# V stored from full transposes, even chunks first, and LayerNorms 2 and 3 with statistics of transposed blocks, in a hybrid encoder layer

## The chip, the core and the metric

The kernel runs on one core of one Trainium2 chip. The metric is the device time of one execution in microseconds (us). The core has a matrix engine (TensorE, PE in the rows), a vector engine (DVE), a scalar engine (ACT), GpSimd (POOL), and a sync engine (SP), from which nearly all transfers of this kernel are issued. Each engine works through its own instructions in order and waits for the others at semaphores.

## The reference

One encoder layer is applied to two groups of requests, each a sequence of 512 tokens with 1024 features, with shared weights, in float32.

```
x = LN(alpha*x + 0.5*SwiGLU_1(x))
h = x @ W_in                       # columns of MLA, of RWKV-7 and of two gates
A = MLA(h_q, h_kv) @ P_mla ; B = RWKV7_bidir(h_rwkv) @ P_rwkv
x = LN(alpha*x + (sig(g_A)*A + sig(g_B)*B) @ W_o)      # LayerNorm 2
x = LN(alpha*x + CrossAttn(x, LN(mem)))                # LayerNorm 3
x = LN(alpha*x + 0.5*SwiGLU_2(x))

# RWKV-7, forward and backward in time, a state S of 64x64 in each of 8 heads
Sa = S @ a_t
S  = S * w_t + outer(Sa, b_t) + outer(v_t, k_t)
y_t = S @ r_t
```

The LayerNorm takes mean and variance of each token over its 1024 features.

## The kernel before

Activations lie transposed: features on the 128 partitions, the 512 tokens of a group along the free axis, so that 1024 features are eight tiles ("rows") of 128x512 per group. A product in nearly full precision is three matmuls of rounded operands: each operand is split into a high and a low part (`xh`, `xl` for activations, `whl` for both parts of a weight), and `Bank.prod` issues high*high, high*low and low*high into one PSUM bank. `Bank.mm` is L215 of the profile, `Bank.tr`, a transpose on PE against the identity `cc`, is L220. The eight PSUM banks go round under three tags, four under "a", two each under "b" and "c". `split` makes the two parts, by a cast on ACT and a subtraction on DVE or GpSimd; `whl` rows are those of weights.

The stages follow each other: SwiGLU 1 (0 to about 700 us, with LayerNorm 1), the projections and MLA (to about 1212), the recurrence (to about 1765), the gated mix (to 1800), W_o with LayerNorm 2 (to 1925), cross attention with LayerNorm 3 (to about 2069), SwiGLU 2 and LayerNorm 4.

The stage before the recurrence runs over four pairs of heads `h` (64 features of each of two heads fill the 128 partitions; a pair is called a head below, as its code counts them so). For each it projects k, r and v for both groups, and between the projections `attend` runs the softmax attention of MLA, whose tiles are `sm_p` and `pt`. The tile of v (`t`, in the rows `sh`, the shifted projection) and its copy with time reversed (`tr`, in the rows `sq`) are turned by `crossed` (L249): the two 64-row halves `e` of the tile are handled apart, chunk by chunk of 64 tokens, the lower half by a matmul with the identity and the upper half by a transpose, so that the halves change places. A copy on DVE or ACT takes the bank to `st`, which is stored to `d_v`.

The recurrence works on eight chunks of 64 tokens. For each head, `front` (L1612) loads v into `uv` (zero in the halves that a block structure leaves out), and r, k, the decays and so on into three `ld` tiles for each group; ACT takes exponentials of the decays (`pp`, `ip`), DVE multiplies them in (`ar`, `bk`), and PE forms `phi`. Then a triangular inverse is built by DVE (`dw`, `tm`, `lw`), turned (`xt`, `ct`) and finished on PE and ACT (`qt`). `chunks` (L1751) runs the eight chunks in turn, each with a state `gs` and `sn`. `sums_in` (L1837) loads v once more (`vt`) and the gate (`gt`), and `sums` applies the head's normalization and gate. Between all these steps `fill` takes pieces of other work, `beside`: projections for the branch gates with their weights `wraw`, whose results `t` are stored to `d_gate`, the memory's projections, and MLA's output.

LayerNorms 2 and 3 are objects of `RowNorm` (L366): each finished row is squared on ACT and added to two running sums, the plain one on GpSimd for group 0 and on DVE for group 1, the squares on DVE (`ln_s`). `stats` multiplies both sums by a column of 1/1024 on PE. LayerNorms 1 and 4 use `BlockNorm` (L394), whose loop is

```
for j in range(4):
    b = Bank(k, self.tags[0])
    for i in range(4):
        b.tr(b.t[:, i * P : i * P + P], self.y(4 * half + i)[:, j * P : j * P + P], k.ident)
    nc.vector.bn_stats(out=self.bn[:, j, half], in_=b.t)
```

so half of a token's features (four rows) is turned into one bank for each block of 128 tokens, and DVE takes its statistics. `Norm.spread` turns mean and rstd back into rows.

`FfnWeights` loads and splits the weights of a SwiGLU, with sums of them for a fast matrix product; `ahead(n)` makes the next n of them early.

The order of instructions on each engine isn't the program's. A scheduler lays the instructions out by simulated times, buffers and priorities, and a change in one place can move others nearby. Waits are on the data and on buffers becoming free; SP's transfers are issued one after the other in its order.

## Time and profile before

| what | value |
|---|---|
| median of 3 runs | 2743.46 us (2743.14 to 2744.37) |
| profiled execution | 2749.23 us, span 2747.4 us |
| granted clock of PE over the span | 0.971 |
| instructions | 41481 |
| PE busy | 2597.5 us, 95% |
| DVE busy | 2118.7 us, 77% |
| ACT busy | 1090.2 us, 40% |
| chain that ended last | PE 54%, DVE 11%, ACT 3%, DMA 2% of the span |

A row of a timeline gives the start from the span's beginning, the duration, the engine, the line of the program, the operation, the tile written and the tiles read, shapes, a count of like instructions, and in square brackets the idle time in front with what ended it. PE's instructions are pipelined, so durations of neighbours overlap; the distance from one start to the next is what a piece takes. SPq rows are the issue of transfers on SP's queue. The row of a group has the count, the sum of the busy time and the mean in ns, then the idle time in front. A window's row has its start and end, its length, the busy time of PE, of its weight loads, DVE, ACT and POOL (with counts), the granted clock, the share of the transfer engines and GB/s.

### The profile page before, as it was taken

The numbers are of one execution on the slowest core, as the hardware profiler recorded it, in microseconds if no ns is written. First come the engines' busy times: TensorE is split into PE (matmuls) and PEld (weight loads), VectorE is DVE, ScalarE is ACT, GpSimd is POOL, SyncE is SP. The second block draws the span as 40 slices with busy tenths as digits, with TensorE's granted clock in tenths as the row PEclk, the third lists the DMA queues.
The fourth block names the chain that finished last, engine by engine and source line by source line (L and its number), as shares of the span: only waits on it lengthen the run. The fifth ranks groups of instructions, "written<-read, shape, count | busy, mean of one in ns | idle before, by whom it ended". The sixth has DMA issues, their size and how long they took to land.

```text
span 2747.4 us, 41481 instructions
## 1 busy us (share of the span) xinstructions
PE 2597.5 (95%) x15600; PEld 2074.1 (75%) x15600; DVE 2118.7 (77%) x3745; ACT 1090.2 (40%) x2004; POOL 699.2 (25%) x479
## 2 busy tenths in 40 slices
PE   8999999999999999997989888999999999999996
PEld 7888887787767777776677676777777888887784
DVE  7888887999466777758475768657788888887988
ACT  5344332222453555444443433224554433342222
POOL 0233332443200001133123331103031323232443
PEclk9999999999999999998999898999999999999998
DMA  4344337671244333343434353541102433347751
GB/s 173 123 154 161 146 135 297 237 264 64 92 171 157 114 97 112 115 139 136 132 110 128 119 179 116 166 157 46 47 31 81 165 143 139 141 173 266 275 200 65
DMA packets 164200, 396.08 MB, mean 144 GB/s; under 512 B 41056, under 2 KB 47456, under 8 KB 164000
## 3 DMA queue, kind: packets, MB, share of 16 engines
q1 hardware_dynamic: 164000, 393.43, 40.9%
q8 instruction: 124, 2.03, 0.3%
q14 instruction: 76, 0.62, 0.1%
HBM read 259.41 MB, written 133.96 MB: 143 GB/s over the span
## 4 chain that ended last, share of the span: by engine, by line
PE 54%; DVE 11%; issue 3%; ACT 3%; DMA 2%; POOL 1%; SPq 0%; POOLq 0%; ACTq 0%; DVEq 0%
PE ps L215 51%; PE ps L220 3%; DVE whl L179 1%; DVE dw L179 1%; DVE x L179 1%; DVE z L179 1%; DVE rs L179 1%; DVE phi L179 1%; DVE tm L179 1%; DVE ln_s L179 1%; DMA ld<-d_rw 1%; DVE wt L179 0%; ACT whl L245 0%; DMA d_q<-st 0%; POOL ln_z L357 0%
## 5 line engine op out<-in xcount | busy, mean ns | idle before, releaser
L215 PE MATMUL ps<-xo,whl 128*128 128x512 f32 x3792 | 899.3, 396 | 14.1 <-DVE z L179 8.5
L215 PE MATMUL ps<-xh,whl 128*128 128x512 f32 x2688 | 889.3, 402 | 15.7 <-ACT xh L245 11.4
L215 PEld LDWEIGHTS ps<-xo,whl 128*128 128x128 f32 x3792 | 712.9, 189 | 185.7 <-DVE z L179 6.7
L215 PEld LDWEIGHTS ps<-xh,whl 128*128 128x128 f32 x2688 | 508.1, 190 | 132.0 <-ACT xh L245 13.0
L215 PE MATMUL ps<-xl,whl 128*128 128x512 f32 x1344 | 536.5, 399 | 1.4 <-POOL xl L246 1.4
L179 DVE TENSOR_TENSOR whl<-wraw,whl 128x512 fp32r<-128x512 f32 (+4 forms) x269 | 280.4, 1052 | 53.2 <-ACT whl L245 52.7
L245 ACT CAST whl<-wraw 128x512 fp32r<-128x512 f32 (+4 forms) x314 | 219.7, 711 | 247.2 <-PE ps L215 226.4
L215 PEld LDWEIGHTS ps<-xl,whl 128*128 128x128 f32 x1344 | 255.9, 190 | 56.4 <-POOL xl L246 2.7
L712 POOL TENSOR_TENSOR s<-s,up 128x512 f32<-128x512 f32 x80 | 116.4, 1455 | 624.0 <-DVE up L179 399.7
L245 ACT CAST whl<-wt 128x512 fp32r<-128x512 f32 (+3 forms) x280 | 148.5, 555 | 272.5 <-PE ps L215 160.7
L179 DVE TENSOR_TENSOR whl<-wt,whl 128x512 fp32r<-128x512 f32 (+3 forms) x280 | 215.5, 791 | 11.5 <-ACT whl L245 11.4
L246 POOL TENSOR_TENSOR whl<-wraw,whl 128x1024 fp32r<-128x1024 f32 x45 | 109.4, 2433 | 385.8 <-ACT whl L245 353.3
L245 ACT CAST hop<-s 128x512 fp32r<-128x512 f32 x128 | 79.5, 621 | 246.1 <-POOL s L712 180.3
L179 DVE TENSOR_TENSOR hop<-s,hop 128x512 fp32r<-128x512 f32 x128 | 121.4, 949 | 58.3 <-ACT hop L245 50.7
L179 DVE SCALAR_TENSOR_TENSOR x<-ps,x 128x512 f32<-128x512 f32 x184 | 124.5, 683 | 53.6 <-PE ps L215 53.0
L179 DVE TENSOR_TENSOR wt<-wraw 128x512 f32<-128x512 f32 (+3 forms) x140 | 109.9, 785 | 1.0
L179 DVE TENSOR_TENSOR wt<-wraw,wt 128x512 f32<-128x512 f32 (+3 forms) x140 | 102.8, 734 | 4.6 <-DMA wraw<-in_wf_dram 2.6
L610 POOL TENSOR_TENSOR x<-x,s 128x512 f32<-128x512 f32 x48 | 70.6, 1476 | 129.4 <-DVE x L179 129.4
L246 POOL TENSOR_TENSOR xl<-x,xh 128x512 fp32r<-128x512 f32 x48 | 66.8, 1420 | 98.2 <-ACT xh L245 97.9
L179 DVE TENSOR_TENSOR p<-ps,p 128x512 f32<-128x512 f32 x120 | 82.2, 685 | 7.2 <-PE ps L215 4.0
L610 POOL TENSOR_TENSOR x<-x,z 128x512 f32<-128x512 f32 x48 | 71.2, 1485 | 52.8 <-DVE x L179 49.2
L215 PE MATMUL ps<-mh,whl 128*128 128x512 f32 x256 | 81.1, 397 | 1.3 <-ACT whl L245 1.3
(328 smaller groups left out, 3715.9 us busy)
## 6 DMA issues: line engine op xcount, KB each, us to landing
d_h<-hop SPq DMA_DIRECT2D x140, 512.0 KB, 2.6
xo<-d_h SPq DMA_DIRECT2D x140, 512.0 KB, 7.2
wraw<-in_wf_dram SPq DMA_DIRECT2D x95, 512.0 KB, 3.4
wraw<-in_wa_dram SPq DMA_DIRECT2D x57, 512.0 KB, 3.5
wraw<-in_wb_dram SPq DMA_DIRECT2D x32, 512.0 KB, 3.4
wraw<-in_wf_dram SPq DMA_DIRECT2D x36, 384.0 KB, 3.7
ld<-d_rw SPq DMA_DIRECT2D x24, 512.0 KB, 4.8
d_gate<-t SPq DMA_DIRECT2D x32, 256.0 KB, 2.3
```

Of the source, the lines that this page charges most:

```text
L179: inst = f(*args, **kw)
L215: self.last = order(k.tc, k.nc.tensor.matmul(out, a, b, start=start, stop=stop), self.last)
L220: self.last = order(self.k.tc, self.k.nc.tensor.transpose(out, a, ident), self.last)
L245: nc.scalar.copy(hi, src)
L246: (low or nc.vector).tensor_tensor(out=lo, in0=src, in1=hi.bitcast(F32), op=ALU.subtract)
L610: eng.tensor_tensor(out=y[r, c], in0=y[r, c], in1=u, op=ALU.add)
L712: nc.gpsimd.tensor_tensor(out=s[:, i], in0=s[:, i], in1=up[:, i], op=ALU.mult)
```

## The change

The turned v is made by four full 128x128 transposes in place of `crossed`. A block of 128 tokens holds two chunks, an even one on the lower partitions and an odd one on the upper. The copy to `st` reorders the free axis so that the two halves `e` of the features come apart, each with its four blocks. As the halves of one chunk's pair no longer lie on opposite partitions, the loads of `uv` and `vt` go by the parity `r` of the chunk: 16 loads of 64x256 in place of 8 of 64x512 for `uv`, and 8 of 64x4x64 in place of 2 of 128x8x64 for `vt`. In `uv` the even chunks come first; `AT` says where a chunk stands, and `chunks` reads `uv[..., AT[i]]` for `uv[..., i]`.

LayerNorms 2 and 3 become `BlockNorm`s, with the tags "c" for the turned blocks and "b" or "c" for the spread rows in LayerNorm 2, and "a" or "c" and "b" or "c" in LayerNorm 3. A half is added when its fourth row is done. The pool of SwiGLU 2's weight sums is opened earlier, and three of its weights are asked for within the second group's rows of cross attention.

```diff
-class RowNorm(Norm):
-    def add(self, n):
-        nc, y = self.k.nc, self.y(n)
-        if n == 0:
-            self.s1, self.s2 = self.tile("ln_s1", 2), self.tile("ln_s2", 2)
-        sq = self.tile("sq", 4) if n else self.s2
-        nc.scalar.activation(out=sq, in_=y, func=AF.Square)
-        if n:
-            eng = nc.gpsimd if self.tags[0] == "c" else nc.vector
-            eng.tensor_tensor(out=self.s1, in0=self.s1 if n > 1 else self.y(0), in1=y, op=ALU.add)
-            nc.vector.tensor_tensor(out=self.s2, in0=self.s2, in1=sq, op=ALU.add)
-    def stats(self):
-        k, nc, sb = self.k, self.k.nc, self.sb
-        st = Bank(k, self.tags[0])
-        for o, t in enumerate((self.s1, self.s2)):
-            for b in range(4):
-                st.mm(st.t[:, 4 * o + b : 4 * o + b + 1], t[:, b * P : b * P + P], k.mean)
-        m = sb.tile([P, 3, 4], F32, name="ln_m", tag="ln_m", bufs=2)
-        mean, var, sq = m[:, 0], m[:, 1], m[:, 2]
-        nc.vector.tensor_copy(m[:, 0:2], st.t[:, 0:8].rearrange("p (a b) -> p a b", b=4))
-        nc.vector.scalar_tensor_tensor(out=sq, in0=mean, scalar=-1.0, in1=mean, op0=ALU.mult, op1=ALU.mult)
-        nc.vector.scalar_tensor_tensor(out=var, in0=sq, scalar=LN_EPS / ALPHA**2, in1=var, op0=ALU.add, op1=ALU.add)
-        Norm.spread([self], mean, var)
@@ -1186,11 +1156,14 @@
                     t = shifted(proj(w, g), 5 + 3 * h)
                     tr = tmp("sq", 2)
                     nc.scalar.copy(tr, t[:, ::-1])
+
                     for d, src in ((0, t), (1, tr)):
                         b = aux()
-                        crossed(b, k, lambda e, c: src[64 * e : 64 * e + 64, c * C : c * C + C])
+                        for i in range(4):
+                            b.tr(b.t[:, i * P : i * P + P], src[:, i * P : i * P + P], k.ident)
                         vt = tmp("st", 2)
-                        (nc.scalar.copy if d else nc.vector.tensor_copy)(vt, b.t)
+                        (nc.scalar.copy if d else nc.vector.tensor_copy)(
+                            vt.rearrange("p (e b v) -> p e b v", e=2, v=C), b.t.rearrange("p (b e v) -> p e b v", e=2, v=C))
                         nc.sync.dma_start(out=d_v[h][g][:, d], in_=vt)
                     attend(3)
@@ -1309,21 +1282,23 @@
     y32 = keep.tile([P, G, KT, T], F32, name="x32")
     x32 = [y32[:, g] for g in range(G)]
-    def norms_of(i):
-        return [RowNorm(k, sb, lambda n, g=g: x32[g][:, n], f"ln{i}_g", f"ln{i}_b", "cb"[g] * 2) for g in range(G)]
+    def norms_of(i, *tags):
+        return [BlockNorm(k, sb, lambda n, g=g: x32[g][:, n], f"ln{i}_g", f"ln{i}_b", tags[g]) for g in range(G)]
     for q in range(4):
         for g in range(G):
             nc.sync.dma_start(out=x32[g][:, 2 * q : 2 * q + 2], in_=d_x1[g][:, 2 * q : 2 * q + 2])
+    ow = ctx.enter_context(pool("ow", "right"))
     wb_pool = cross.enter_context(pool("wb", "right"))
     st.use((wp, 3, 2), (wb_pool, 2, 0), (wp, 3, 2), (wb_pool, 2, 0), (wp, 3, 2))
     def sum_row(norm, g, n, b, f):
         y = x32[g][:, n]
         nc.vector.scalar_tensor_tensor(out=y, in0=b.t, scalar=f, in1=y, op0=ALU.mult, op1=ALU.add)
-        norm.add(n)
-
-    norms = norms_of(2)
+        if n % 4 == 3:
+            norm.add(n // 4)
+
+    norms = norms_of(2, ("c", "b"), ("c", "c"))
     w = []
     def mix_rows(g, ns):
@@ -1340,11 +1315,11 @@
         for g in range(G):
             mix_rows(g, range(n0, n0 + 4))
             if (n0, g) == (4, 0):
-                norms[0].stats()
+                BlockNorm.stats(norms[:1], False)
     x2 = [None, None]
     for g in range(G):
         if g:
-            norms[g].stats()
+            BlockNorm.stats(norms[1:], False)
         x2[g] = (acts if g else others)(KT, "x")
         norms[g].apply(x2[g])
@@ -1430,22 +1405,23 @@
     kvs[1] = memory_of(1)
     xo[1] = acts(4, "co")
     w = [st.blocks(4) for _ in range(KT)]
-    norms = norms_of(3)
+    norms = norms_of(3, ("a", "b"), ("c", "c"))
     both(attend(1), out_rows(0))
-    norms[0].stats()
-    for _ in out_rows(1):
-        pass
+    BlockNorm.stats(norms[:1], False)
+    fw = FfnWeights(k, wf2, [(wp, 3)] * 3 + [(ow, 1)], [(wp, 2)] * 2 + [(ow, 1)], ow)
+    for i, _ in enumerate(out_rows(1)):
+        if i % 4 == 3 and i > 4:
+            fw.ahead(1)
     x3 = [None, None]
     for g in range(G):
         if g:
-            norms[g].stats()
+            BlockNorm.stats(norms[1:], False)
         x3[g] = acts(KT, "x")
         norms[g].apply(x3[g])
     cross.close()
-    ow, of = ctx.enter_context(pool("ow", "right")), ctx.enter_context(pool("of"))
-    fw = FfnWeights(k, wf2, [(wp, 3)] * 3 + [(ow, 1)], [(wp, 2)] * 2 + [(ow, 1)], ow)
+    of = ctx.enter_context(pool("of"))
     ln = []
     def sums2():
 ...
+    AT = (0, 4, 1, 5, 2, 6, 3, 7)
@@ -1619,9 +1597,10 @@
         self.ar = []
         for g in range(G):
             for d in range(2):
-                src = self.d_v[h][g][:, d].rearrange("p (c v) -> p c v", v=C)
+                src = self.d_v[h][g][:, d].rearrange("p (e b v) -> p e b v", e=2, v=C)
                 for e in range(2):
-                    nc.sync.dma_start(out=uv[UP[1 - e], d, e, g], in_=src[UP[1 - e]])
+                    for r in range(2):
+                        nc.sync.dma_start(out=uv[UP[1 - e], d, e, g, 4 * r : 4 * r + 4], in_=src[UP[r], e])
                     nc.gpsimd.memset(uv[UP[e], d, e, g], 0.0)
         for g in range(G):
             ld = [self.t4("ld") for _ in range(3)]
@@ -1786,12 +1765,12 @@
             for e, x, d, g, j in each():
                 p.mm(p.t[UP[e], x * C : x * C + C], phi[UP[e], e, j + i, 0:C], gs[UP[e], x])
             for e, cp in ((0, nc.scalar.copy), (1, nc.vector.tensor_copy)):
-                cp(uv[UP[e], :, e, :, i], p.t[UP[e], 0 : 4 * C].rearrange("p (d g v) -> p d g v", d=2, g=G))
+                cp(uv[UP[e], :, e, :, AT[i]], p.t[UP[e], 0 : 4 * C].rearrange("p (d g v) -> p d g v", d=2, g=G))
             self.fill(beside / 16)
             if i < NC - 1:
                 p = self.bank("c")
                 for e, x, d, g, j in each():
-                    p.mm(p.t[UP[e], x * C : x * C + C], bt[:, e, j + i], uv[:, d, e, g, i])
+                    p.mm(p.t[UP[e], x * C : x * C + C], bt[:, e, j + i], uv[:, d, e, g, AT[i]])
                 sn = sb.tile([P, 4, C], F32, name="sn", tag="sn", bufs=2)
                 pc = pcs[:, i].rearrange("p g d -> p d g").unsqueeze(3).to_broadcast([P, 2, G, C])
                 v4 = lambda t: t.rearrange("p (d g) v -> p d g v", d=2)
@@ -1841,9 +1820,10 @@
         v4 = vt.rearrange("p (c g v) -> p g c v", g=G, v=C)
         g5 = gt.rearrange("p (b r g v) -> p g r b v", b=4, r=2, g=G)
         for g in range(G):
-            nc.sync.dma_start(out=v4[:, g], in_=self.d_v[h][g][:, 0].rearrange("p (c v) -> p c v", v=C))
+            src = self.d_v[h][g][:, 0].rearrange("p (e b v) -> p e b v", e=2, v=C)
             for e in range(2):
                 for r in range(2):
+                    nc.sync.dma_start(out=v4[UP[1 - e], g, r:NC:2], in_=src[UP[r], e])
                     col = h * P + e * C
                     nc.sync.dma_start(out=g5[UP[1 - e], g, r], in_=self.d_g[g][UP[r], :, col : col + C])
         return vt, gt, z
```

Where v is turned, PE's order in the first head was, and is now, as follows. `sh` is the tile in forward time, `sq` the one with time reversed, `sm_p` a tile of the softmax, `xh` and `xl` the projection's activations.

```order
L215 MATMUL ps<-xh_5608,whl 128x512
L215 MATMUL ps<-cc,sh 64x64 x8
L220 MATMUL ps<-cc,sh 64x64 x2
L220 MATMUL ps<-cc,sm_p 128x128 x4
L220 MATMUL ps<-cc,sh 64x64 x6
L215 MATMUL ps<-cc,sq 64x64 x8
L220 MATMUL ps<-cc,sq 64x64 x8
L215 MATMUL ps<-xh_5608,whl 128x512
```

```order
L215 MATMUL ps<-xh_5606,whl 128x512
L220 MATMUL ps<-cc,sh 128x128 x3
L220 MATMUL ps<-cc,sm_p 128x128 x4
L220 MATMUL ps<-cc,sh 128x128
L220 MATMUL ps<-cc,sq 128x128 x4
L215 MATMUL ps<-xh_5606,whl 128x512
```

Sixteen small instructions for each tile become four; what stands around them stays.

At the start of the first head's front, SP's order before and now; `lx` is a constant of the recurrence, `d_gate` the stores of gate tiles, `ld<-d_rw_0` the loads for group 0, `ld<-d_rw_1` those for group 1.

```order
L1598 DMA lx<-in_lnx_dram 128x512
L1624 DMA uv<-d_v_0_83 64x512 x4
L1624 DMA uv<-d_v_1_84 64x512 x4
L1629 DMA ld<-d_rw_0_75 128x1024 x3
L945 DMA d_gate_66<-t 128x512
L945 DMA d_gate_67<-t 128x512
L141 DMA wraw<-in_wa_dram 128x1024
L945 DMA d_gate_68<-t 128x512
L1629 DMA ld<-d_rw_1_76 128x1024 x3
```

```order
L1576 DMA lx<-in_lnx_dram 128x512
L1603 DMA uv<-d_v_0_83 64x256 x8
L1603 DMA uv<-d_v_1_84 64x256 x8
L1608 DMA ld<-d_rw_0_75 128x1024 x3
L915 DMA d_gate_66<-t 128x512
L915 DMA d_gate_67<-t 128x512
L915 DMA d_gate_68<-t 128x512
L141 DMA wraw<-in_wa_dram 128x1024
L1608 DMA ld<-d_rw_1_76 128x1024 x3
```

Sixteen loads of uv stand ahead of group 0's ld where eight did, and the store of gate tile 68 is still ahead of group 1's ld. That tile, the last `t` below, is made on ACT at the same place:

```order
L1645 ACTIVATE pp_10252<-ld 128x8x64
L1646 ACTIVATE ip<-ld 128x512
L1653 COPY pcs<-pp_10252 128x8
L1645 ACTIVATE pp_10253<-ld 128x8x64
L1653 COPY pcs<-pp_10253 128x8
L944 ACTIVATE t<-ps,sc_b_gate 128x512
L1650 COPY bk<-bk 64x8x64
L1646 ACTIVATE ip<-ld 128x512
```

```order
L1624 ACTIVATE pp_10058<-ld 128x8x64
L1625 ACTIVATE ip<-ld 128x512
L1632 COPY pcs<-pp_10058 128x8
L1624 ACTIVATE pp_10059<-ld 128x8x64
L1632 COPY pcs<-pp_10059 128x8
L1629 COPY bk<-bk 64x8x64
L1625 ACTIVATE ip<-ld 128x512
L914 ACTIVATE t<-ps,sc_b_gate 128x512
L1629 COPY bk<-bk 64x8x64
```

The gate tile has moved behind a copy of `bk` and a second exponential.

Near the end of LayerNorm 3's group 1 on PE, where `xh` and `xl` belong to SwiGLU 2's first products for group 0:

```order
L215 MATMUL ps<-xh_18875,whl 128x512 x2
L215 MATMUL ps<-mean,ln_s_18746 128x1 x4
L215 MATMUL ps<-xl_18876,whl 128x512
L215 MATMUL ps<-xh_18875,whl 128x512
L215 MATMUL ps<-xh_18877,whl 128x512
L215 MATMUL ps<-mean,ln_s_18747 128x1 x4
```

```order
L215 MATMUL ps<-xh_18809,whl 128x512
L220 MATMUL ps<-cc,x_16734 128x128 x2
L215 MATMUL ps<-xl_18810,whl 128x512
L215 MATMUL ps<-xh_18809,whl 128x512 x2
L215 MATMUL ps<-xl_18810,whl 128x512
L215 MATMUL ps<-xh_18809,whl 128x512 x2
L215 MATMUL ps<-xl_18810,whl 128x512
L220 MATMUL ps<-cc,x_16734 128x128 x4
```

In place of two sets of mean products, transposes of the rows stand among the first products of SwiGLU 2.

More of the change, by code (lines that the diff above doesn't have):

```diff
@@ L864 @@
     nc.vector.memset(k.half, 0.5)
-    k.mean = cp.tile([P, 1], F32, name="mean")
-    nc.vector.memset(k.mean, 1.0 / D)
     vc = cp.tile([P, NVEC], F32, name="vc")
@@ L1751, in chunks @@
     def chunks(self, h, beside, early_rows):
-        k, sb, nc, UP = self.k, self.sb, self.k.nc, self.UP
+        k, sb, nc, UP, AT = self.k, self.sb, self.k.nc, self.UP, self.AT
         phi, uv, bt, ar, pcs = self.phi, self.uv, self.bt, self.ar, self.pcs
@@ L1770, in given @@
             for e, x, d, g, j in each():
-                p.mm(p.t[UP[e], x * C : x * C + C], phi[:, e, j + i, 0:C], uv[:, d, e, g, i], x == 0, i == 0 and x == 3)
+                p.mm(p.t[UP[e], x * C : x * C + C], phi[:, e, j + i, 0:C], uv[:, d, e, g, AT[i]], x == 0, i == 0 and x == 3)
             return p
@@ L1805, in chunks @@
                 o = py.t[UP[1 - e], x * C : x * C + C]
-                py.mm(o, phi[:, e, j + i, C : 2 * C], uv[:, d, e, g, i], i == 0 and x == 0, x == 3)
+                py.mm(o, phi[:, e, j + i, C : 2 * C], uv[:, d, e, g, AT[i]], i == 0 and x == 0, x == 3)
             self.fill(beside / 16)
```

## The prediction

> **What bounds the kernel now.** I read the totals first, then stretches of the span, then what TensorE waits for in the stretches that the change touches.
>
> ```profile
> PE 2597.5 (95%) x15600; PEld 2074.1 (75%) x15600; DVE 2118.7 (77%) x3745; ACT 1090.2 (40%) x2004; POOL 699.2 (25%) x479
> 870.00:1150.00 280.00, 279.55 (x1614) 216.51 (x1613) 216.56 (x533) 138.44 (x272) 30.74 (x27) 1.00 0.36 116
> 1215.00:1300.00 85.00, 69.93 (x588) 58.35 (x588) 64.10 (x162) 36.93 (x59) 29.37 (x19) 0.90 0.48 162
> 1620.00:1765.00 145.00, 125.97 (x1703) 101.77 (x1704) 105.53 (x256) 42.06 (x78) 24.24 (x21) 0.91 0.45 140
> 2018.00:2069.00 51.00, 46.86 (x213) 36.75 (x211) 49.77 (x80) 31.05 (x47) 24.71 (x16) 1.00 0.13 42
> ```
>
> In a window's row the third to seventh figures are the busy time of PE, its weight loads, DVE, ACT and POOL. The share over the span (95%) hides three regimes. From 870 to 1150, where V is transposed, PE has no free time (279.55 of 280 us) at clock 1.00, and DVE has 63 us of 280 left: there a microsecond of PE work is a microsecond. In the recurrence (1215 to 1765) PE idles 15 of 85 us in the first head and 19 of 145 in the last. From 2018 to 2069, the end of LayerNorm 3, DVE is the full one (49.77 of 51). What PE waits for in the first head, and the long waits of the third and fourth:
>
> ```profile
> PE ps L215 <- DVE xt L179: 7.3, 1, 7.3
> PE ps L215 <- DVE xt L179: 6.1, 1, 6.1
> PE ps L215 <- DVE xt L179: 8.5, 1, 8.5
> ```
>
> Each head ends its inverse with PE out of fill work, waiting for the chain that began with the loads. What comes late at a head's front therefore comes out late at its end.
>
> **A. V's transposes: PE loses 20.3 us where it is full.** `crossed` (eight 64x64 fp32 products, two records each, and eight 64x64 transposes) runs 16 times: 4 heads, 2 groups, 2 directions.
>
> ```profile
> 925.43 1.14 PE L215 MATMUL ps<-cc,sq 64*64 64x64 f32 x16
> 927.06 0.50 PE L215 MATMUL ps<-xh,whl 128*128 128x512 f32 x1
> 929.47 0.60 PE L220 MATMUL ps<-cc,sm_p 128*128 128x128 f32 x4
> 929.82 0.48 PE L215 MATMUL ps<-xl,whl 128*128 128x512 f32 x1
> ```
>
> From start to start, which is what PE gives up, a crossing takes 927.06 - 925.43 = 1.63 us, and four full transposes of another tile take 929.82 - 929.47 = 0.35, say 0.36. The gain is 16 x 1.27 = 20.3 us. The copies out keep their size (128x512; their order is in the access pattern), so I price them at nothing; they lie under PE's work on DVE and ACT, and without that cover DVE's free 63 us would have to hold them at whatever they grow by. If the softmax chain takes over as bound in places, less is kept: 14 at the low end, 20.5 at the high one.
>
> The Trainium skill (TensorE: Matmul & The Clock Gate, Part 4: PE-mode transpose) states about 275 ns for a full transpose in a kernel. The rows decide against adding it up: four go by in 0.35 us. Added up, the 64 new ones would take 17.6 us as an estimate from that page, and A would be worth 8.5.
>
> **B. More loads on SP's queue: the recurrence begins later.** uv goes from 8 loads of 64x512 to 16 of 64x256 per head, vt from 2 to 8.
>
> ```profile
> 1207.90 0.33 SPq L141 DMA_DIRECT2D wraw<-in_wa_dram  x1
> 1215.48 4.94 SPq L1624 DMA_DIRECT2D uv<-d_v  x8
> 1220.52 1.48 SPq L1629 DMA_DIRECT2D ld<-d_rw  x3
> ld<-d_rw SPq DMA_DIRECT2D x24, 512.0 KB, 4.8
> 1224.74 0.69 ACT L944 ACTIVATE t<-ps,sc_b_gate 128x512 f32<-128x512 f32 x1 [3.82 <-PE ps L215]
> 1225.33 0.62 ACT L1645 ACTIVATE pp<-ld 128x512 f32<-128x512 f32 x1
> 1236.91 0.63 ACT L1645 ACTIVATE pp<-ld 128x512 f32<-128x512 f32 x1 [2.30 <-DMA ld<-d_rw]
> 1238.27 2.10 DVE L179 TENSOR_TENSOR ar<-ld,pp 128x512 f32<-128x512 f32 x3 [2.39 <-DMA ld<-d_rw]
> ```
>
> An issue of uv holds SP for 4.94 / 8 = 0.62 us. Half the columns could halve that; the lower bound is the 0.33 of a weight load, and the upper the 0.80 of gt below. I take 0.62: a weight load moves four times uv's bytes and is cheaper, so size is not what it pays for. The first ld, issued 1220.52, lands 4.8 later, at 1225.3, and its reader `pp` starts at 1225.33: no slack. Eight more issues in front of it make the first front 5.0 us late. That delay also reaches the second group's ld: SP waits ahead of it to store a gate tile `t`, and in the new order that tile's activation is behind `bk` and `ip` on ACT (shown with the change), which belong to the late front. In the old order ACT did the tile first. So nothing of the 5.0 is made up: **head 0: +5.0**.
>
> ```profile
> 1374.94 1.89 SPq L1624 DMA_DIRECT2D uv<-d_v  x3
> 1377.55 0.38 SPq L1629 DMA_DIRECT2D ld<-d_rw  x1
> 1383.78 1.28 DVE L179 TENSOR_TENSOR bk<-ld,ip 128x512 f32<-128x512 f32 x2
> 1502.18 5.65 SPq L1624 DMA_DIRECT2D uv<-d_v  x8
> 1511.10 0.38 SPq L1629 DMA_DIRECT2D ld<-d_rw  x1
> 1518.35 1.27 DVE L179 TENSOR_TENSOR bk<-ld,ip 128x512 f32<-128x512 f32 x2
> 1643.88 0.58 SPq L1629 DMA_DIRECT2D ld<-d_rw  x1
> 1650.75 1.29 DVE L179 TENSOR_TENSOR bk<-ld,ip 128x512 f32<-128x512 f32 x2
> ```
>
> In the other heads the last ld has slack before its reader `bk`: 1383.78 - 1377.55 - 4.8 = 1.4 us, 2.4 and 2.1. In head 1 three uv loads stood behind a store that SP waits for, now eight do; so ld comes 3.1, 5.0 and 5.0 later: +1.7, +2.6, +2.9. DVE takes its queue in order, so the rest of the front, the xl splits of the fill work, and PE wait behind `bk`. Sum of the fronts: 5.0 + 1.7 + 2.6 + 2.9 = 12.2 us.
>
> ```profile
> 1438.96 1.35 SPq L1844 DMA_DIRECT2D vt<-d_v  x2
> 1440.40 2.06 SPq L141 DMA_DIRECT2D wraw<-in_wa_dram  x1
> 1442.57 6.44 SPq L1848 DMA_DIRECT2D gt<-d_g  x8
> 1459.68 1.04 ACT L245 CAST whl<-wraw 128x1024 fp32r<-128x1024 f32 x1
> ```
>
> The new vt loads are of gt's form (64 partitions in pieces), 0.80 each, so vt and gt take 12.8 us where they took 7.8. Their readers stand later in DVE's new order, behind the whole of chunk 1, so I take 0, with up to 2 us a head if not. The weight load issued between them (1440.40) slides behind all sixteen, to about 1452, and was cast at 1459.68: 7 us are left, more than its landing takes at the price of ld (4.8). The lower bound of B is +2 (issues of 0.33 leave uv at its 5 us), the upper +22, or +30 with the sums late (worked out below).
>
> The Trainium skill (DMA: Bandwidth & Descriptors, Rules for kernel authors) advises against cutting a transfer into disjoint partition halves, since the parts serialize. The vt and gt rows agree: 0.68 us for a whole tile's issue, 0.80 for a half's.
>
> **C. LayerNorms 2 and 3.** Removed: squares on ACT, sums on DVE and POOL, and the mean products.
>
> ```profile
> L179 DVE TENSOR_TENSOR ln_s<-ln_s,sq 128x512 f32<-128x512 f32 x28 | 27.6, 987 | 4.5 <-ACT sq L374 4.0
> L179 DVE TENSOR_TENSOR ln_s<-ln_s,x 128x512 f32<-128x512 f32 x12 | 9.2, 768 | 0.1
> L215 PE MATMUL ps<-mean,ln_s 128*128 128x1 f32 x64 | 8.0, 246 | 1.1 <-POOL ln_s L377 0.6 <-DVE ln_s L179 0.5
> L179 DVE BATCH_NORM_STATS2 ln_b<-ps 128x6 f32<-128x512 f32 x32 | 21.2, 688 | 2.5 <-PE ps L220 2.3
> 2051.53 0.65 PE L220 MATMUL ps<-cc,ln_m 128*128 128x128 f32 x4 [1.04 <-DVE ln_m L179]
> 2066.01 0.50 PE L215 MATMUL ps<-xh,whl 128*128 128x512 f32 x1 [1.45 <-ACT s L681]
> 2069.39 0.51 PE L215 MATMUL ps<-xh,whl 128*128 128x512 f32 x1 [1.71 <-DVE s L179]
> ```
>
> PE gains 128 full transposes (2 norms, 2 groups, 32) at 0.35 / 4 = 11.2 us and loses the mean products, at most their 8.0 us busy, about 6.5 in PE's time since their records overlap: +4.7. DVE loses 36.8 us and gains 32 statistics of 0.69, 22.0, and 16 small combinations, about 3: some 12 us less, half of it at LayerNorm 3 where DVE is full. With that I expect most of PE's waits there (1.04, 1.45, 1.71, and 1.1 before the mean products: 5.3) to go: -4. The transposes of each half wait for its fourth row, which DVE has just finished, and products stand behind them on PE: +1. FFN2's first weights are now split within LayerNorm 3; that work is moved, on the DVE time set free. C comes to +1.7, between -4 (no new waits, all old ones gone) and +6 (the transposes wait, nothing goes).
>
> **The sum.** -20.3 + 12.2 + 1.7 = -6.4. The profiled execution lasted 2749.23 us (span 2747.4), so it would take 2742.8; against the median of 2743.46 that is **2737**.
>
> **The rivals.** *The loads are hidden:* issues of half the width take 0.33, or the first head's fill covers the late front. For it speaks that the new pieces carry half the bytes; against it PE's waits for xt. B is then +2: -20.3 + 2 + 1.7 = -16.6, 2727.
>
> *The recurrence pays more than the stage before it gains (slower):* SP is the bound of every front, each new issue costs gt's 0.80. Then the fronts are late by 16 x 0.80 - 4.94 = 7.9, by 5.0 - 1.4 = 3.6 in head 1 (five eighths of it), and by 12.8 - 5.65 - 2.4 = 4.8 and 7.9 - 2.1 = 5.8: 22. With vt and gt 2 us late at the sums in each head, 30; -20.3 + 30 + 1.7 = +11, 2755; with half of that second part, 2751. It decides from a B above 18.6 us. For it: the interleaved loads of vt and gt; against: uv's rows are steady at 0.62.
>
> *LayerNorm 3's transposes become the wait:* PE's queue is in order, and each group of four needs four rows from a DVE that was full. C is then +6 and more: -2, 2741, no change to be told.
>
> *The change doesn't do what it says:* the V stage is held by DVE's chain once PE is relieved, and only 14 us come: -0.1, 2743. Against it: DVE's 63 free us.
>
> *Transposes add up* (a full one costs its record's own mean): the group of rows of the softmax gives
>
> ```profile
> L220 PE MATMUL ps<-cc,sm_p 128*128 128x128 f32 x320 | 52.0, 277 | 3.7 <-DVE sm_p L179 2.4 <-DVE pt L179 0.8 <-DVE sm_s L179 0.3
> ```
>
> At 0.277 each A is 26.1 - 17.7 = -8.4 and C 35.5 - 6.5 - 3 = +26: +30, 2773. The row of four in 0.35 us is against it. The Trainium skill's figure given under A is nearly this mean.
>
> **How the numbers follow.** A measurement of this kernel tells from no change what exceeds 0.2%, 5.5 us. Chances: forecast 0.43 (2731 to 2741 of its own), loads hidden 0.22, recurrence pays more 0.14, LayerNorm 3 waits 0.12, V stage held 0.07, transposes add up 0.02. The forecast lies just past the bound, so I count two thirds of it as faster, which with the hidden loads makes 0.51; the rest of it, LayerNorm 3's and the V stage's cases make 0.33 of no change, and the two slower rivals 0.16. The range 2725 to 2749 takes in the hidden loads and stops short of the slower rival.
>
> **What would show it.** A: in the V stage four full transposes about 0.36 us from start to start, and the first head's `lx` load about 20 us earlier. B: 16 uv loads in about 10 us, the first ld 5 us later against `lx`, PE's wait for xt in the first head at 11 to 13 us, and the recurrence 10 to 14 us longer. C: no ln_s rows, DVE with free time from LayerNorm 3 on, and w_o to FFN2 within 4 us of before. If uv's issue falls to 0.33 us, or the xt waits do not grow, B is wrong and the time falls towards 2727; if the sums wait for vt, it is wrong the other way.

## The result

The changed kernel took 2729.18 us (median of four runs, 2726.95 to 2733.67), the kernel before 2743.3 in the same series: -14.1 us. The ratio is 0.9937, with a 95% interval from 0.9918 to 0.9955. A second series gave 2733.62 us and 0.9955 (0.9943 to 0.9968). The forecast was 2737, -6.4 us: the right sign, inside the range, and about half of what came, or less. A ratio here is not that of the two medians: by its ratio the first series is at -17 us and the second at -12. The differences in us of the experiments below are all taken from ratios. One execution of experiment 7's kernel (7427 us) and one of the kernel before (10199 us) were far slower than all others and are left out. The profiled execution after took 2733.67 us, with a span of 2731.9 against 2747.4.

The totals of the page after:

```profile
PE 2576.3 (94%) x15344; PEld 2067.5 (76%) x15344; DVE 2098.0 (77%) x3742; ACT 1073.5 (39%) x1972; POOL 682.5 (25%) x465
```

The windows that answer those of before (the V stage, the first head, the last head, LayerNorm 3), with the same columns:

```profile
865.00:1145.00 280.00, 276.83 (x1369) 214.84 (x1368) 225.17 (x550) 146.79 (x287) 36.78 (x29) 0.99 0.39 121
1195.00:1280.00 85.00, 69.66 (x589) 58.52 (x589) 64.38 (x162) 34.92 (x56) 25.56 (x17) 0.88 0.51 169
1612.00:1760.00 148.00, 123.30 (x1642) 99.51 (x1641) 107.26 (x249) 40.76 (x76) 24.87 (x20) 0.88 0.43 131
2011.00:2056.00 45.00, 44.46 (x212) 35.92 (x210) 42.44 (x77) 27.52 (x40) 20.74 (x15) 1.00 0.08 24
```

PE is still full in the V stage, and idles more in the recurrence than before (24.7 of 148 us in the last head, for 19 of 145). At LayerNorm 3 it is now full (44.46 of 45), where it was not (46.86 of 51); DVE has a little more room than before (42.44 of 45, for 49.77 of 51).

**Where the time went.** Two spans say little as long as stages gain and lose, so I cut all profiles at the starts of the same instructions: the first and last score product of MLA (`kp,qp`), the issue of `lx`, the first product of W_o (`mh,whl`), the first score product of cross attention (`xk`), its last output product (`coh`), and the first and last `xo` product of SwiGLU 2 (of a group of like instructions in a row, the first). Lengths in us, one profile each; the kernels are explained with the experiments:

| kernel | to `kp` | V stage | to `lx` | recurrence, mix | W_o, LN2 | cross | LN3 | SwiGLU 2 | rest |
|---|---|---|---|---|---|---|---|---|---|
| before | 886.6 | 317.1 | 11.3 | 583.8 | 119.9 | 118.3 | 62.1 | 614.8 | 33.5 |
| after | 881.1 | 302.4 | 11.9 | 598.6 | 123.1 | 112.9 | 57.3 | 611.4 | 33.3 |
| after, again | 881.8 | 300.9 | 11.9 | 598.6 | 122.9 | 114.4 | 57.3 | 610.8 | 33.7 |
| V part alone | 880.7 | 300.8 | 11.9 | 594.1 | 119.9 | 115.0 | 62.0 | 614.9 | 32.8 |
| LayerNorms, early weights | 882.1 | 317.2 | 11.2 | 585.1 | 122.6 | 112.9 | 57.2 | 611.2 | 33.6 |
| LayerNorms alone | 884.1 | 317.2 | 11.3 | 586.0 | 122.7 | 112.6 | 58.9 | 610.7 | 33.6 |
| before, uv cut | 881.9 | 317.0 | 11.2 | 599.2 | 121.0 | 115.4 | 62.0 | 614.9 | 33.6 |
| before, 32 bytes lower | 885.7 | 317.2 | 11.2 | 584.5 | 119.5 | 114.9 | 61.9 | 610.7 | 33.6 |
| after, 32 bytes higher | 883.4 | 300.9 | 11.9 | 596.0 | 122.9 | 114.7 | 57.5 | 614.9 | 33.2 |
| after, uv merged | 878.7 | 302.3 | 11.9 | 583.6 | 123.9 | 112.9 | 57.2 | 610.9 | 33.7 |
| after, uv behind ld | 880.8 | 299.3 | 11.9 | 588.7 | 122.1 | 112.9 | 57.2 | 610.8 | 33.1 |
| after, 64 bytes higher | 884.8 | 301.0 | 11.9 | 599.4 | 124.0 | 113.1 | 57.3 | 613.9 | 33.7 |
| after, uv merged and behind ld | 878.6 | 300.9 | 11.9 | 588.9 | 122.0 | 112.8 | 57.2 | 613.3 | 33.9 |
| the same in the first head alone | 879.8 | 302.2 | 11.9 | 586.7 | 123.5 | 114.4 | 57.3 | 611.4 | 33.2 |

The first column holds no changed work, and varies by 8 us from profile to profile: that is what one profile's whole span can be off by. The profile of before has its longest value, and its longest cross attention. The other columns repeat within 1 to 2 us where the program is the same, except the recurrence (some 5 us), the V stage (3 us) and cross attention (up to 3 us).

What differs in these last two is PE's granted clock, which in these traces is 1.00 or, for stretches of some us, 0.50. The changed kernel has such a stretch in its V stage, from the one product that has to wait there (shown below) on:

```profile
1051.40:1058.20 6.80, 6.80 (x25) 5.81 (x26) 3.92 (x12) 0.78 (x2) 0.00 (x0) 0.50 0.31 97
```

It lasts 6.8 us here, 3.4 us in the second profile of the changed kernel, and is missing in experiment 8: at half speed they cost 3.4, 1.7 and 0 us, which is what tells 302.4, 300.9 and 299.3 apart. Cross attention, whole, in the kernel before, in experiment 5 (the old LayerNorms too), and in the second and the first profile of the changed kernel:

```profile
1918.66:2036.93 118.27, 110.66 (x568) 89.58 (x568) 94.12 (x253) 60.29 (x154) 14.86 (x11) 0.96 0.10 32
1918.03:2032.91 114.88, 107.17 (x569) 87.10 (x569) 94.04 (x253) 60.18 (x154) 14.85 (x11) 0.99 0.11 33
1916.09:2030.50 114.41, 108.87 (x600) 90.37 (x599) 93.73 (x257) 57.34 (x146) 8.18 (x7) 0.99 0.15 43
1917.01:2029.90 112.89, 107.41 (x601) 89.23 (x599) 93.73 (x257) 57.43 (x146) 8.21 (x7) 1.00 0.15 44
```

At the same clock (0.99) the old and the new LayerNorms are only half a us apart; the changed kernel itself shows both 0.99 and 1.00.

### The profile page after: what moved, and what is told of

Read it like the earlier page. It is cut to its first block, busy times and chain, and to the rows that moved or that the text cites. A ratio compares the mean times of both kernels' runs of the same rounds, so it can differ in the third digit from the quotient of the medians.

```text
span 2731.9 us, 40963 instructions
## 1 busy us (share of the span) xinstructions
PE 2576.3 (94%) x15344; PEld 2067.5 (76%) x15344; DVE 2098.0 (77%) x3742; ACT 1073.5 (39%) x1972; POOL 682.5 (25%) x465
## 5 line engine op out<-in xcount | busy, mean ns | idle before, releaser
L215 PE MATMUL ps<-xo,whl 128*128 128x512 f32 x3792 | 896.9, 395 | 14.8 <-DVE z L179 9.1
L215 PEld LDWEIGHTS ps<-xh,whl 128*128 128x128 f32 x2688 | 509.3, 191 | 128.4 <-ACT xh L245 13.5
L179 DVE TENSOR_TENSOR whl<-wt,whl 128x512 fp32r<-128x512 f32 (+3 forms) x280 | 214.8, 788 | 13.5 <-ACT whl L245 13.5
```

The source lines that it names most:

```text
L179: inst = f(*args, **kw)
L215: self.last = order(k.tc, k.nc.tensor.matmul(out, a, b, start=start, stop=stop), self.last)
```

## The experiments

**1. The V part alone.** The changed kernel with the old LayerNorms in both places, and the weights of SwiGLU 2 made where they were.

```diff
-    norms = norms_of(3, ("a", "b"), ("c", "c"))
+    norms = norms_of(3)
     both(attend(1), out_rows(0))
-    BlockNorm.stats(norms[:1], False)
-    fw = FfnWeights(k, wf2, [(wp, 3)] * 3 + [(ow, 1)], [(wp, 2)] * 2 + [(ow, 1)], ow)
-    for i, _ in enumerate(out_rows(1)):
-        if i % 4 == 3 and i > 4:
-            fw.ahead(1)
+    norms[0].stats()
+    for _ in out_rows(1):
+        pass
...
```

> The change's V part alone: full transposes, the new storage order and the loads of uv and vt that follow from it; LayerNorms 2 and 3 and the weights of SwiGLU 2 as before. From the two profiles I read off that the V part brings about 20 us up to the load of lx and that the recurrence gives 15 of them back, so this theory expects -5 us (2738). The rival, that the LayerNorms' part moved nothing and the difference there is the run's own variation, expects the whole -14 (2729).

Ratio 0.9981 (0.9969 to 0.9992), -5.2 us. The first theory holds. The V stage is 16 us shorter, the recurrence 10 longer.

**2. The LayerNorm part alone, with the early weights.** The changed kernel with the V part undone, its loads too.

```diff
-                        for i in range(4):
-                            b.tr(b.t[:, i * P : i * P + P], src[:, i * P : i * P + P], k.ident)
+                        crossed(b, k, lambda e, c: src[64 * e : 64 * e + 64, c * C : c * C + C])
 ...
```

> The LayerNorm part alone, with the weights of SwiGLU 2 asked for early; V and its loads as before. First theory: -9 us (2734), of which some 5 between the first and the last rows of cross attention and 5 at LayerNorm 3 and SwiGLU 2's start, with LayerNorm 2 at +2. The rival: within 2 us of the kernel before. The prediction's term was +1.7.

Ratio 0.9957 (0.9942 to 0.9973), -11.8 us. By its ratio this part is worth more than the one on which the forecast rested, though the two intervals overlap a little; the prediction's +1.7 is refuted. LayerNorm 2 costs 3 us, and the gain lies in LayerNorm 3 and, unexpectedly, in SwiGLU 2 itself, whose work is the same. Cross attention is shorter too, for the most part by the granted clock.

**3. The LayerNorms without the early weights.** Experiment 2 with the weights made where they were before.

```diff
     BlockNorm.stats(norms[:1], False)
-    fw = FfnWeights(k, wf2, [(wp, 3)] * 3 + [(ow, 1)], [(wp, 2)] * 2 + [(ow, 1)], ow)
-    for i, _ in enumerate(out_rows(1)):
-        if i % 4 == 3 and i > 4:
-            fw.ahead(1)
+    for _ in out_rows(1):
+        pass
...
     cross.close()
+    ow, of = ctx.enter_context(pool("ow", "right")), ctx.enter_context(pool("of"))
+    fw = FfnWeights(k, wf2, [(wp, 3)] * 3 + [(ow, 1)], [(wp, 2)] * 2 + [(ow, 1)], ow)
```

> LayerNorms 2 and 3 by transposed blocks, but SwiGLU 2's weights made where they were before, and their pool opened there. If DVE's relief is what pays, it brings most of what the LayerNorm part with early weights brings: -5 to -9 us. If the early weights pay, -2 to +2 us, with PE's waits of some 3 us at SwiGLU 2's first products still there.

Ratio 0.9969 (0.9956 to 0.9983), -8.5 us. Most of it comes without early weights; the intervals of 2 and 3 overlap. What PE waits for from the end of LayerNorm 3 on, in the kernel before (three of its rows), in this one and in the changed one:

```profile
PE ps L215 <- DVE s L179: 1.7, 1, 1.7
PE ps L215 <- ACT s L681: 1.4, 1, 1.4
PE ps L220 <- DVE ln_m L179: 1.0, 1, 1.0
```

```profile
PE ps L220 <- DVE x L179: 1.3, 1, 1.3
PE ps L215 <- DVE s L179: 0.8, 1, 0.8
```

```profile
PE ps L215 <- ACT s L653: 0.6, 1, 0.6
```

The waits fall from 4.4 us (0.3 for a weight included) to 2.1 and to 0.6: statistics on blocks take away those for ln_m, for ACT's `s` and for the weight and half of the one for DVE's `s`, and bring a new one, of a transpose for its row `x` (1.3); early weights take most of the rest.

**4. The loads of uv cut, in the kernel before.**

```diff
                 for e in range(2):
-                    nc.sync.dma_start(out=uv[UP[1 - e], d, e, g], in_=src[UP[1 - e]])
+                    for r in range(2):
+                        nc.sync.dma_start(out=uv[UP[1 - e], d, e, g, 4 * r : 4 * r + 4], in_=src[UP[1 - e], 4 * r : 4 * r + 4])
```

> The kernel before with each load of uv cut in two halves of its columns (16 loads of 64x256 per head for 8 of 64x512) and nothing else. It measures the issue's price by itself. If SP's queue sets the fronts: the first ld 5.0 us later against lx, +8 to +13 us in all (2752 to 2756). If the late front is covered: +0 to +3 us.

Ratio 1.0043 (1.0027 to 1.006), +11.8 us, with nothing else changed. SP's queue in this kernel, and in the changed one, at the first head:

```profile
1210.09 0.44 SPq L1598 DMA_DIRECT2D lx<-in_lnx_dram  x1
1210.62 10.06 SPq L1625 DMA_DIRECT2D uv<-d_v  x16
1220.77 1.48 SPq L1630 DMA_DIRECT2D ld<-d_rw  x3
1229.98 1.75 SPq L1630 DMA_DIRECT2D ld<-d_rw  x3
```

```profile
1195.35 0.54 SPq L1576 DMA_DIRECT2D lx<-in_lnx_dram  x1
1195.93 10.07 SPq L1603 DMA_DIRECT2D uv<-d_v  x16
1206.11 1.48 SPq L1608 DMA_DIRECT2D ld<-d_rw  x3
1215.30 1.75 SPq L1608 DMA_DIRECT2D ld<-d_rw  x3
```

A half load costs SP the same 0.63 us as a whole one did (0.62), and the first ld follows lx by 10.7 and 10.8 us where it was 5.6 (1214.94 for lx, 1220.52 for ld). This gives the recurrence 15.4 us more, and the changed kernel's has 14.8 more: the cut loads explain its loss within the 5 us by which this column varies, and vt needs no part in it.

**5 and 6. Where the tiles lie.** In experiments 2 and 3 SwiGLU 2 was 4 us shorter, though nothing in it had changed. The constant column of 1/1024, which the change removes with its only user, occupied 32 bytes of each partition ahead of all tiles from the left; without it they all lie 32 bytes lower. (The addresses are those of the program's layout; no profile shows them.) Experiment 5 moves that constant in the kernel before (first diff), experiment 6 puts it back in the changed one, without a use (second diff).

```diff
-    k.half = cp.tile([P, 1], F32, name="half")
+    hm = cp.tile([P, 2], F32, name="half")
+    k.half = hm[:, 0:1]
-    k.mean = cp.tile([P, 1], F32, name="mean")
+    k.mean = hm[:, 1:2]
```

```diff
     nc.vector.memset(k.half, 0.5)
+    k.mean = cp.tile([P, 1], F32, name="mean")
+    nc.vector.memset(k.mean, 1.0 / D)
```

> The kernel before, with the constant column of 1/1024 put into the second place of the tile of the constant one half, and nothing else: the same instructions in the same order, but every tile that is laid out behind the constants lies 32 bytes lower, as in the changed kernel, where that constant is gone. The profiles show 642 matmuls in 150 us at the start of SwiGLU 2 wherever the constant has its own tile and 647 where it is gone. If the place of the tiles is the cause: 647 here too, and -4 to -7 us (0.9975 to 0.9985). If the LayerNorms are: 642 and no change.

> The changed kernel with the constant column kept in its own tile, unused, so that all tiles lie 32 bytes higher, where they lay before. Place theory: 642 matmuls in 150 us of SwiGLU 2, and 4 to 7 us slower than the changed kernel, -7 to -10 us against the kernel before. LayerNorm theory: 647 and -14 us.

The windows of 150 us that begin some 2 us behind the first of SwiGLU 2's `xo` products: before, V part alone, and experiment 6 (the constant in its own tile); then LayerNorms alone, the changed kernel, and experiment 5 (no tile of its own).

```profile
2101.00:2251.00 150.00, 150.00 (x642) 120.59 (x641) 128.75 (x172) 58.28 (x102) 43.57 (x29) 1.00 0.40 143
```

```profile
2086.00:2236.00 150.00, 150.00 (x642) 120.60 (x641) 128.77 (x172) 58.38 (x103) 43.16 (x29) 1.00 0.41 142
```

```profile
2089.00:2239.00 150.00, 150.00 (x642) 120.59 (x641) 128.73 (x172) 58.29 (x103) 43.34 (x29) 1.00 0.41 143
```

```profile
2094.00:2244.00 150.00, 150.00 (x647) 121.59 (x647) 129.96 (x173) 58.85 (x103) 44.14 (x29) 1.00 0.41 144
```

```profile
2089.00:2239.00 150.00, 150.00 (x647) 121.59 (x646) 130.09 (x173) 58.37 (x103) 44.66 (x29) 1.00 0.41 144
```

```profile
2096.00:2246.00 150.00, 150.00 (x647) 121.60 (x646) 129.93 (x174) 58.86 (x103) 43.90 (x29) 1.00 0.41 144
```

Behind the window's length stands PE's busy time with its count. PE is never idle in any of the six and the granted clock is 1.00, yet it starts 642 or 647 matmuls: 150 us by the count is 0.2336 or 0.2318 us for one. The place decides it, by two pairs of kernels (experiment 5 and the kernel before, experiment 6 and the changed one) that differ in nothing else. SwiGLU 2 is 4.1 us shorter in experiment 5 (610.7 for 614.8), which as a whole is at 0.9989 (0.998 to 0.9998), -3.0 us: a little less than expected. In SwiGLU 1 there is hardly any of it: from 200 to 350 us PE starts 654 matmuls in the kernel before and 655 in experiment 5. Experiment 6 has 614.9 us again and is at 0.9977 (0.9966 to 0.9988), -6.3 us, between 6 and 11 us slower than the changed kernel in its two series (0.9955 and 0.9937). SwiGLU 2 shows 3.5 to 4 us of this; the rest is not placed, and within the intervals.

**7. Two directions in one load.** The changed kernel, with the loads of uv merged over `d`: 8 loads per head, in two pieces of 256 columns.

```diff
-            for d in range(2):
-                src = self.d_v[h][g][:, d].rearrange("p (e b v) -> p e b v", e=2, v=C)
-                for e in range(2):
-                    for r in range(2):
-                        nc.sync.dma_start(out=uv[UP[1 - e], d, e, g, 4 * r : 4 * r + 4], in_=src[UP[r], e])
+            src = self.d_v[h][g].rearrange("p d (e b v) -> p d e (b v)", e=2, v=C)
+            for e in range(2):
+                for r in range(2):
+                    to = uv[UP[1 - e], :, e, g, 4 * r : 4 * r + 4].rearrange("p d c v -> p d (c v)")
+                    nc.sync.dma_start(out=to, in_=src[UP[r], :, e])
```

> The changed kernel with the two directions of one load of uv in one transfer: again 8 loads per head, each of 64x2x256, with the same bytes and the same pieces of 256 columns. If SP pays by the load (0.62 us), the fronts are as early as before and this is 8 to 11 us faster than the changed kernel (2718 to 2721, ratio about 0.990). If it pays by the piece, each takes 1.2 us and nothing changes (0.994).

Ratio 0.9903 (0.9888 to 0.9919), 2717.55 us: 9 to 14 us faster than the changed kernel in its two series, 27 faster than before. SP pays by the load:

```profile
1193.49 5.07 SPq L1603 DMA_DIRECT2D uv<-d_v  x8
1198.66 1.48 SPq L1609 DMA_DIRECT2D ld<-d_rw  x3
1208.41 1.75 SPq L1609 DMA_DIRECT2D ld<-d_rw  x3
```

Eight loads of twice the bytes in 5.07 us, 0.63 each, and the recurrence is at 583.6 us, as before the change (583.8). vt still has its eight loads per head here, so they cost nothing that this column could show.

**8. uv behind ld.** The changed kernel, with the 16 half loads, each group's placed behind its ld loads.

```diff
         for g in range(G):
             ld = [self.t4("ld") for _ in range(3)]
             for i in (2, 0, 1):
                 nc.sync.dma_start(out=ld[i], in_=self.d_rw[h][g][:, 2 * i : 2 * i + 2])
+            for d in range(2):
+                src = self.d_v[h][g][:, d].rearrange("p (e b v) -> p e b v", e=2, v=C)
+                for e in range(2):
+                    for r in range(2):
+                        nc.sync.dma_start(out=uv[UP[1 - e], d, e, g, 4 * r : 4 * r + 4], in_=src[UP[r], e])
...
```

> The changed kernel with each group's 16 half loads of uv placed behind that group's ld loads in the program instead of in front of all. If the late ld is what the recurrence pays for: the first ld follows lx at once, 10 us earlier than in the changed kernel and 5 earlier than in the one before, PE's wait for xt in the first head falls below 7 us, and the time by 10 to 15 us against the changed kernel (2714 to 2719). If other things bound the fronts, it stays within 4 us of it.

Ratio 0.991 (0.9897 to 0.9922), 2720.36 us: 7 to 12 us faster than the changed kernel in its two series, at the lower end of what was expected or below it. The waits for the end of the inverse in the first head, in the changed kernel, in experiment 7 and here:

```profile
1274.41 3.62 PE L215 MATMUL ps<-xt,phi 32*32 32x32 f32 x128 [11.93 <-DVE xt L179]
```

```profile
1270.63 3.62 PE L215 MATMUL ps<-xt,phi 32*32 32x32 f32 x128 [9.40 <-DVE xt L179]
```

```profile
1262.61 3.59 PE L215 MATMUL ps<-xt,phi 32*32 32x32 f32 x127 [3.43 <-DVE xt L179]
```

From 11.93 us to 3.43, the fewer the loads ahead of ld, in these three. But by the second head 6 of these 8 us are lost again: from the first xt product to the second head's it takes 1429.81 - 1291.12 = 138.7 us before the change and 144.8 here. Why the second head loses them was not tried further.

**9 to 12. The changed kernel again; 64 bytes; and two ways to combine 7 and 8.**

Experiment 10 adds two unused constants to the changed kernel, 11 has the merged loads of 7 in the place of 8, and 12 the merged loads behind ld in the first head alone. The first diff is that of 10, the second what 12 adds to 11.

```diff
     nc.vector.memset(k.half, 0.5)
+    pad0 = cp.tile([P, 1], F32, name="pad0")
+    nc.vector.memset(pad0, 1.0)
+    pad1 = cp.tile([P, 1], F32, name="pad1")
+    nc.vector.memset(pad1, 1.0)
```

```diff
+        for g in range(G if h else 0):
+            src = self.d_v[h][g].rearrange("p d (e b v) -> p d e (b v)", e=2, v=C)
...
-            for e in range(2):
+            for e in range(0 if h else 2):
```

> The changed kernel itself, so that it stands beside the others on one chip. 0.9937 of the kernel before again (2728 to 2730), and 4 to 10 us faster than its twin with the tiles 32 bytes higher, which was at 0.9977.

> The changed kernel with two unused constants, so that the tiles lie 64 bytes higher than in it and 32 higher than in the kernel before. If what counts is where a tile starts within 64 bytes: 647 matmuls in 150 us of SwiGLU 2, and the changed kernel's time. If it is only that the tiles lie lower, or within 128 bytes: 642, and the time of the one with a single unused constant.

> Both: 8 loads of uv per head, each group's behind its ld. The two single steps came to 0.990 and 0.991 of the kernel before. Where the ld is the bound of every front they add: 0.988 (2712). Placed behind ld, uv cost 6 us between the first and the second head; if that is from the place and not from the number, this stays at 0.990.

> 8 loads of uv per head, behind ld in the first head only and in front of it in the others. It keeps the 5 us that the late place gained in the first head and avoids the 6 us that it lost in the second: 0.9885 of the kernel before (2713 to 2715), 3 to 5 us faster than with the loads in front everywhere. If the first head's gain is used up by the second anyway, 0.990.

The changed kernel came to 0.9955 (0.9943 to 0.9968), a little above the 0.9937 that was expected; with 64 bytes to 0.9963 (0.9951 to 0.9975), and its SwiGLU 2 starts neither 647 nor 642:

```profile
2093.00:2243.00 150.00, 150.00 (x645) 120.21 (x644) 129.34 (x173) 58.59 (x103) 43.59 (x29) 1.00 0.41 144
```

So a rule of place within 64 bytes is not shown, only that the place counts. The combinations came to 0.9913 (0.99 to 0.9927) and 0.9914 (0.9902 to 0.9926): no better than 7 alone, where 0.988 and 0.9885 had been hoped for. The first head's gain is used up by the second, and 7, with the lowest ratio, is the simplest of the three.

## Why the prediction was right, and where it was wrong

**A, V's transposes: right.** Four transposes take what the row of the softmax's four said:

```profile
923.74 0.60 PE L220 MATMUL ps<-cc,sh 128*128 128x128 f32 x4
924.09 0.48 PE L215 MATMUL ps<-xh,whl 128*128 128x512 f32 x1
```

0.35 us here, 0.35 to 0.44 over ten of them. The rival of transposes that add up is out, by the same rows. The stage is 14.7 to 17.8 us shorter instead of 20.3. The 3.1 us between these are the granted clock's, as shown above: 17.8 is the profile without a stretch at half clock, and the forecast had the clock at 1.00 throughout. Of the 2.5 us that are left, one product that now waits is 1.9,

```profile
1051.28 1.74 PE L215 MATMUL ps<-cc,sq 128*128 128x2 f32 x8 [1.92 <-DVE sq L179]
```

and 2.1 are fill work that the scheduler moved into the stage (nine matmuls of 128x512 more than before, at 0.23 us; the recurrence has nine fewer), which is not lost. So the transposes themselves gained what was forecast, or a little more. A stretch at half clock begins within 2 us of that wait in eight of the nine profiles that have the wait; that the wait brings it on is not shown, as experiment 8 has the one without the other. The first head's `lx` came 19.6 us earlier for "about 20", which is in part luck: 5.5 of it lie ahead of the V stage, in unchanged work. That DVE holds the stage, the fourth rival, is seen in this one wait only.

**B, the loads: right in its cause, shown by experiments 4 and 7, and in its sum partly by luck.** 12.2 us forecast; 14.8 measured in both profiles of the changed kernel, 10.3 to 15.6 over all kernels with 16 loads ahead of ld, 0 with 8. Of its steps: the issue's price was right to 0.01 us, and the first ld came 5.2 us later for 5.0. The second ld came 20.0 us behind lx for 16.4 (1231.32 before), 3.6 later rather than 5.0, so "nothing of the 5.0 is made up" was wrong: the first head's inverse (its first `xt` product) was only 2.9 us late against lx. From there to the next heads' and to W_o the changed kernel loses 0.3, 3.6, 4.1 and 3.9 us, and in its second profile 3.7 in the first head, then -0.9, 6.5, 5.3 and 0.2; the forecast had 5.0, then 1.7, 2.6, 2.9 and nothing. The lateness is paid, but not head by head as priced. Nor is all of it waiting. The recurrence from lx to W_o, before and after:

```profile
1214.94:1798.74 583.80, 510.85 (x6068) 412.79 (x6066) 393.78 (x884) 224.86 (x408) 146.03 (x94) 0.91 0.44 141
1195.35:1793.91 598.56, 515.94 (x6059) 417.96 (x6057) 392.33 (x883) 224.99 (x407) 142.81 (x92) 0.89 0.44 137
```

PE's idle time grows by 9.7 us (583.80 - 510.85 to 598.56 - 515.94), and its busy time by 5.1 for nine matmuls less, at a lower granted clock (0.89 for 0.91), which the forecast did not price. The wait for xt, 11.93 us for "11 to 13", agrees by luck: with the cut loads alone (experiment 4) it is 8.41,

```profile
1291.44 3.62 PE L215 MATMUL ps<-xt,phi 32*32 32x32 f32 x128 [8.41 <-DVE xt L179]
```

and with the V part but eight loads (experiment 7) 9.40, for 7.34 before; so a part of it comes with the V part, which fits the nine products that moved out of the recurrence. The first rival, hidden loads, is out. The slower rival's price of 0.80 is out too: gt's issues, from which it came, and the new ones of vt take 0.61 each when they follow each other,

```profile
1429.71 0.61 SPq L1826 DMA_DIRECT2D vt<-d_v  x1
1430.36 0.61 SPq L1828 DMA_DIRECT2D gt<-d_g  x1
1431.02 0.61 SPq L1826 DMA_DIRECT2D vt<-d_v  x1
```

and the loads of vt cost nothing that shows, as forecast. A load of uv takes 0.6 us of the queue whether it carries 64x256, 64x512 or 64x2x256, and experiment 7 gets the time back by putting more into each; loads of other forms are cheaper (0.33 us for the 128x1024 weight load among the prediction's rows). The Trainium skill advises against cutting a transfer into partition halves (DMA: Bandwidth & Descriptors, Rules for kernel authors). The rows of vt, the one load that the change cuts so, agree: a half's issue takes 0.61 us where a whole tile's took 0.68.

**C, the LayerNorms: wrong, and this is what made the forecast small.** The step that failed is the sum "+4.7 - 4 + 1 = +1.7"; measured, the part alone is -11.8 (-7 to -16). It counted too few of the waits that go, put too high a charge against them, and looked at neither cross attention nor the place of the tiles. By the table, against kernels with the old LayerNorms:

- LayerNorm 2: about +3 us (122.0 to 124.0 for 119.5 to 121.0). That is the price of PE's transposes, of the right size: half of 4.7, and some waits.
- LayerNorm 3: -4.8 us (57.2 to 57.5 with early weights, for 61.9 to 62.1). The term had "-4" for the waits taken away and put half of the transposes' price and a new wait against it. The waits did go (4.4 to 0.6). The charge was too high: only 16 of this norm's 64 transposes stand in the stretch, in the place of 16 mean products, and in the changed kernel no new wait came.
- Cross attention: about -2 (112.6 to 114.7 for 114.9 to 115.4, the kernel before left out), but only about -0.5 at the same granted clock (114.4 to 114.7 for 114.9 to 115.4 at 0.99). I had not looked there. The rows of group 0 are finished within it, and their squares and sums had been on ACT and DVE between the steps of the softmax; PE waited for `sm_p` 3.1 us in the kernel before, 3.1 in experiment 5, and 0.6 after, and a little longer for `xpt` instead. From the kernel of experiment 5:

```profile
PE ps L215 <- ACT xpt L245: 3.2, 5, 0.8
PE ps L220 <- DVE sm_p L179: 1.9, 7, 0.4
PE ps L215 <- ACT sm_p L1475: 1.2, 1, 1.2
```

and the changed one:

```profile
PE ps L215 <- ACT xpt L245: 4.2, 6, 1.0
PE ps L220 <- DVE sm_p L179: 0.4, 1, 0.4
PE ps L215 <- ACT sm_p L1450: 0.2, 1, 0.2
```

By the windows above, at clock 0.99, PE's idle time falls by 2.2 us (7.7 to 5.5) and its work grows by 1.7, with 48 transposes for 16 mean products. Seven of the ten profiles with the new LayerNorms stay at clock 1.00 here and none of the four with the old, but the changed kernel does so in one of its profiles and not in the other; that the change takes the half clock away is not shown.

- SwiGLU 2: -4, from the place of the tiles, which no row of before shows and the diff only by a removed constant. It isn't what the change is about, and would as well have come from moving that constant.

So at the same clock the stages that the term priced come to -2.3 (3 - 0.5 - 4.8) for its +1.7, and SwiGLU 2 brings the larger part. Together these make -8 as the profiles stand, within the interval of the part's timing, and -6 with cross attention at the same clock, just short of it; some of the -11.8 is not placed. The third rival, that PE's transposes wait at LayerNorm 3, is out for the changed kernel, where no wait of theirs is left in that stretch; without the early weights there is one, of 1.3 us.

The parts add up: -5.2 for the V part and -11.8 for the LayerNorms make -17, with -17 and -12 measured by the same measure (-14.1 by the medians) and intervals of 3 to 5 us to each side. That the time fell into the forecast's range owes something to luck: the V part came out 3 us worse than forecast (-5.2 for -20.3 + 12.2 = -8.1) and C 13.5 better, beyond its own bound of -4. Of the 15.5 us between the two profiles' spans, 5.5 lie ahead of the V stage in unchanged work, so those two profiles taken alone would have misled by that much.

## What to carry to other kernels

Price a queue by the number of its transfers, and look at what stands behind them: eight more issues of 0.6 us ahead of a load that starts a chain cost 12 to 15 us over four such chains, and merging loads, bytes unchanged, got it all back. When work is taken off ACT or DVE, look at every stage in which it ran, also as a guest between another's steps, and not only at the end that bears its name. Compare a stage of two profiles at the same granted clock: a stretch at half clock, 3 to 10 us of it in a stage here, can hide or feign an effect of 1 to 5 us. And time a change that adds or removes an allocation against one that only shifts the tiles, before its effect is put down to its work.

## What I had not expected of the hardware

PE without a pause, at granted clock 1.00, issued the same stream of 128x512 matmuls at 0.2336 or 0.2318 us each, 0.8% apart, when all activation tiles were moved by 32 bytes against the weights' tiles in the program's layout; tiles 64 bytes above those of the changed kernel gave 150 / 645 = 0.2326. What within the memory makes the difference is open: no run here tells a conflict of reads by PE from one with DVE's or the transfers' accesses.
